# Products inside a chunk, as 64-token halves and in one run per group: a change to the SSD scan of a hybrid decoder trunk

## The chip, the cores and the metric

The kernel runs on one core of one Trainium2 chip. The metric is device time in microseconds (us) of one execution, the median of several runs. A profile of one execution comes with it: records of PE (TensorE's matmuls), PEld (its weight loads), DVE (VectorE), ACT (ScalarE), POOL (GpSimd) and of the DMA queues.

## The reference

One layer of a decoder trunk with two parallel branches, for 16 meta tokens and 2048 real ones at width 1024, all in float32: `u = RMSNorm(h)`, one projection of `u` to all branch inputs and gates, an SSD branch (Mamba-2), a gated linear attention branch (GLA), a gated merge, an output projection, and a last RMSNorm. The change is in the SSD branch. It has 16 heads of 64 channels in 4 groups; the four heads of a group share `bm` and `cm`, of 128 state features each. In chunks of 128 tokens the reference computes

```
da_cum = jnp.cumsum(da, axis=-1)
decay = jnp.exp(jnp.where(causal, seg, -jnp.inf))     # seg[t,s] = da_cum[t] - da_cum[s]
scores = jnp.einsum('bzthn,bzshn->bhzts', cc, bc)
y_diag = jnp.einsum('bhzts,bzsh,bzshp->bzthp', scores * decay, dtc, xc)
states = jnp.einsum('bzshn,bhzs,bzsh,bzshp->bzhpn', bc, decay_to_end, dtc, xc)
# the state is handed on from chunk to chunk: s = chunk_decay * s + states
y_off = jnp.einsum('bzthn,bzhpn,bhzt->bzthp', cc, prev, jnp.exp(da_cum))
y = y_diag + y_off
```

Then `d_skip * xs` is added, the sum is multiplied by `silu(z)`, and each group of 256 channels is normalised by its root mean square over the group. `y_diag`, the product inside a chunk, needs no state; `y_off` and the state do, chunk by chunk.

## The kernel before, in words

There are two stages. The first goes through the 2048 tokens in 4 blocks of 512 (4 chunks each; block 0 has the meta tokens as well, `m0` is then 16) and does projections, the convolution and both scans; it lasts to about 1310 us in the profile. The second does the gates, the branch products and the output product; the change doesn't touch it.

A block's projections are cut into 48 pieces (one more in the last block). After each piece, `step()` (line 1005) calls every running generator once, the oldest first: scans, gates, sums, loads. With the pieces counted from 0, the scan `ssd_scan(o, g)` of group g begins after piece 6(g+1), and the next one six pieces later. So the work of a scan comes in steps, one behind each piece, and the order of PE and SP is the order in which the program writes them (`manual_schedule`, line 1059); that of DVE, ACT and POOL is laid out by a planner from a model of the times.

The steps of one scan (line 630), before the change:

1. The DMA that brings the first chunk's cumulative sums, spread over all partitions (`cb`, line 628).
2. The scores of all four chunks in one bank (line 660), masked by DVE into `scm` (line 662); then `before(0)`.
3. `before(1)`, then `after(0)`. In block 0 the meta tokens' state (line 653, a product on 16 rows) comes as a step ahead of this one.
4. `before(2)`, `after(1)`.
5. `before(3)`, `after(2)`.
6. `after(3)`.
7. The root mean square of each token's group (`rstd_of`), and the scaling of the four chunks on ACT (line 742).
8. (A step later in group 0 of blocks 1 to 3.) Eight transposes (line 749), an eviction with a weight (line 751), and the store of y.

`before(c)` (line 668) transposes the two feature tiles of x and the one of bm (line 676), and makes out of them: `xdt`, x times dt (line 679); `xw`, x times the decay to the chunk's end (line 681); the start of `yt`, x times d_skip (line 682); `bt` (line 685). ACT makes the four decays `dm` of 128 x 128, and DVE multiplies them by the scores (line 692).

`after(c)` (line 695) has on PE, all in fp32: four products of 128 x 128 by 128 x 64, one a head (line 701, `dm[:, h]` is the stationary side and `xdt[:, h]` the moving one); `cf` by the state (line 702); `bt` by `xw` (line 704). Then POOL multiplies the state by the chunk's decay (line 706), DVE adds the new part (line 707), and DVE makes y in four operations (lines 709 to 714): state part times its decay, plus the inside part, plus `yt`, times the gate `zs`. ACT squares and sums (line 721).

Each scan runs beside the projections, `accum` (lines 221 to 225), whose operands are split into two fp32r parts, three matmuls a product. The buffers that matter: PSUM pools `pj` (3 banks), `pt` (3, transposes) and `pc` (2, the scan's products; GLA uses it too). In SBUF, tag `tok4` (5 buffers) holds the z gates, `yt`, v and the gates' `gmt`; `sq` (5) holds `scm` and `dm`, and the GLA scan's tiles; `c1` (8) holds `xdt`, `xw` and `yo`.

Of the kernel before, what the change touches and what calls it, by code (L numbers as in the profile page):

```python
# [8 lines left out]
F32 = mybir.dt.float32  # L9
# [4 lines left out]
ALU = mybir.AluOpType  # L14

P = 128
# [4 lines left out]
NCH = BLK // P  # L21
# [2 lines left out]
NH = 16  # L24
EPS = 1e-6
NWR = 3
NSQ = 5
NT4 = 5
NACT = 8
NC1 = 8  # L30
# [13 lines left out]
def trunk_kernel(ctx: ExitStack, tc: tile.TileContext, xm, xmt, w_feat, w_tok, w_v3, w_zm, w_br, w_o,  # L44
                 cf32, cmsk, pvec, fnw, hvec, gw2, out):
    nc = tc.nc
# [5 lines left out]
    def mk(pool, shape, dt, tag, **kw):  # L52
        cnt[0] += 1
        return pool.tile(shape, dt, tag=tag, name=f"{tag}_{cnt[0]}", **kw)
# [72 lines left out]
    bpool, wk, sm, const = pool1("bpool", 1), pool1("wk", 2), pool1("sm", 4), pool1("const", 1)  # L127
# [4 lines left out]
    pc = ctx.enter_context(tc.tile_pool(name="pc", bufs=2, space=bass.MemoryType.PSUM))  # L132

    def act_tile(dt=F32):
        return mk(wk, [P, 64 + BLK], dt, "act", bufs=NACT)

    def bank(pool, tag):
        return mk(pool, [P, 512], F32, tag)
# [19 lines left out]
    s_ssd = const.tile([P, SG, 256], F32, name="s_ssd")  # L158
# [319 lines left out]
    def gates(o):  # L478
        m0, tt, chunks, g_all = o.m0, o.tt, o.chunks, o.g_all
        ast = (act_tile(F32R) if m0 else mk(wk, [P, BLK], F32R, "sq", bufs=NSQ))[:48, :tt]  # L480
        for a, n in ([(0, META), (m0, BLK)] if m0 else [(0, BLK)]):
# [148 lines left out]
    def ssd_scan(o, g):  # L630
        m0, ci0 = o.m0, o.ci0
        tkd, tkc, wde, ecu, dec = o.tkd, o.tkc, o.wde, o.ecu, o.dec
        x0, x1, bf, cf = o.feats[g]
        fetch_cb(o, g, 0)
        yield
        hs = slice(4 * g, 4 * g + 4)

        def hb(t, n):
            return t.unsqueeze(2).to_broadcast([n, 4, 64])

        if m0:
            ps = bank(pt, "pt")
            for j, f in enumerate((x0, x1, bf)):
                nc.tensor.transpose(ps[:META, j * P:(j + 1) * P], f[:, :META], ident)
            xw = mk(wk, [P, 4, 64], F32, "c1", bufs=NC1)
            nc.vector.tensor_tensor(xw[:META], ps[:META, :256].rearrange("p (a c) -> p a c", c=64),
                                    hb(wde[:META, 0, hs], META), op=ALU.mult)
            btm = mk(wk, [P, P], F32, "bt")
            nc.scalar.activation(btm[:META], ps[:META, 256:384], AF.Copy)

        def meta_state():
            ps = bank(pc, "pc")
            nc.tensor.matmul(ps[:, :256], btm[:META], xw[:META].rearrange("p a c -> p (a c)"),
                             start=True, stop=True)
            nc.vector.tensor_copy(s_ssd[:, g], ps[:, :256])

        sc = bank(pc, "pc")
        for c in range(NCH):
            a = m0 + c * P
            nc.tensor.matmul(sc[:, c * P:(c + 1) * P], bf[:, a:a + P], cf[:, a:a + P], start=True, stop=True)  # L660
        scm = mk(wk, [P, NCH, P], F32, "sq", bufs=NSQ)
        nc.vector.tensor_tensor(scm, sc.rearrange("p (c t) -> p c t", t=P),
                                tri.unsqueeze(1).to_broadcast([P, NCH, P]), op=ALU.mult)
        yt = mk(wk, [P, NCH, 256], F32, "tok4", bufs=NT4)
        ssq = mk(sm, [P, 4], F32, "ssq")
        held = {}

        def before(c):
            a = m0 + c * P
            ci = ci0 + c  # L670
            if c + 1 < NCH:
                fetch_cb(o, g, c + 1)
            cb = cbs.pop((g, c))
            ps = bank(pt, "pt")
            for j, f in enumerate((x0, x1, bf)):
                nc.tensor.transpose(ps[:, j * P:(j + 1) * P], f[:, a:a + P], ident)  # L676
            px = ps[:, :256].rearrange("p (h c) -> p h c", c=64)
            xdt = mk(wk, [P, 4, 64], F32, "c1", bufs=NC1)
            nc.vector.tensor_tensor(xdt, px, hb(tkd[:, ci, hs], P), op=ALU.mult)
            xw = mk(wk, [P, 4, 64], F32, "c1", bufs=NC1)  # L680
            nc.vector.tensor_tensor(xw, px, hb(wde[:, ci, hs], P), op=ALU.mult)
            nc.vector.tensor_tensor(yt[:, c].rearrange("p (h c) -> p h c", c=64), px,
                                    hb(d_skip[:, hs], P), op=ALU.mult)
            bt = mk(wk, [P, P], F32, "bt")
            nc.scalar.activation(bt, ps[:, 256:384], AF.Copy)
            dm = mk(wk, [P, 4, P], F32, "sq", bufs=NSQ)
            with behind() if o.b == 0 else nullcontext():
                for h in range(4):
                    nc.scalar.activation(dm[:, h], cb[:, h], AF.Relu, scale=-1.0,
                                         bias=tkc[:, ci, 4 * g + h:4 * g + h + 1])  # L690
                nc.scalar.activation(dm, dm, AF.Exp, scale=-1.0)
            convd[:] = [nc.vector.tensor_tensor(dm, dm, scm[:, c].unsqueeze(1).to_broadcast([P, 4, P]), op=ALU.mult)]
            held[c] = xdt, xw, bt, dm

        def after(c):
            a = m0 + c * P
            ci = ci0 + c
            xdt, xw, bt, dm = held.pop(c)
            py = bank(pc, "pc")
            for h in range(4):  # L700
                nc.tensor.matmul(py[:, h * 64:(h + 1) * 64], dm[:, h], xdt[:, h], start=True, stop=True)  # L701
            nc.tensor.matmul(py[:, 256:512], cf[:, a:a + P], s_ssd[:, g], start=True, stop=True)  # L702
            pst = bank(pc, "pc")
            nc.tensor.matmul(pst[:, :256], bt, xw.rearrange("p a c -> p (a c)"), start=True, stop=True)  # L704
            sv = s_ssd[:, g].rearrange("p (h c) -> p h c", c=64)
            nc.gpsimd.tensor_tensor(sv, sv, hb(dec[:, ci, hs], P), op=ALU.mult)
            nc.vector.tensor_tensor(s_ssd[:, g], s_ssd[:, g], pst[:, :256], op=ALU.add)
            yo = mk(wk, [P, 4, 64], F32, "c1", bufs=NC1)
            nc.vector.tensor_tensor(yo, py[:, 256:512].rearrange("p (h c) -> p h c", c=64),
                                    hb(ecu[:, ci, hs], P), op=ALU.mult)  # L710
            yof = yo.rearrange("p a c -> p (a c)")
            nc.vector.tensor_tensor(yof, yof, py[:, 0:256], op=ALU.add)
            nc.vector.tensor_tensor(yof, yof, yt[:, c], op=ALU.add)
            nc.vector.tensor_tensor(yt[:, c], yof, o.zs[g][:, c], op=ALU.mult)
            if not m0:
                square(c)

        def square(c):
            with behind() if m0 else nullcontext():
                jk = mk(wk, [P, 256], BF16, "junk", bufs=1)  # L720
                nc.scalar.activation(jk, yt[:, c], AF.Square, accum_out=ssq[:, c:c + 1])

        before(0)
        yield
        if m0:
            meta_state()
            yield
        for c in range(1, NCH):
            before(c)
            if m0 and c > 1:  # L730
                square(c - 2)
            after(c - 1)
            yield
        if m0:
            square(NCH - 2)
        after(NCH - 1)
        yield
        if m0:
            square(NCH - 1)
        r = rstd_of(ssq, 4, 1.0 / 1024)  # L740
        for c in range(NCH):
            nc.scalar.activation(yt[:, c], yt[:, c], AF.Identity, scale=r[:, c:c + 1])
        yield
        if not m0 and not g:
            yield
        for j in range(2):
            ps = bank(pt, "pt")
            for c in range(NCH):
                nc.tensor.transpose(ps[:, c * P:(c + 1) * P], yt[:, c, j * P:(j + 1) * P], ident)
            yo = mk(wk, [P, BLK], F32, "gg", bufs=4)  # L750
            nc.scalar.activation(yo, ps, AF.Identity, scale=hsw[:, 2 * g + j:2 * g + j + 1])
            nc.scalar.dma_start(y_left[0][o.b][2 * g + j], yo)
# [51 lines left out]
    def gla_scan(o, h, last=False):  # L804
# [33 lines left out]
        def level_in(half):  # L838
# [8 lines left out]

            ex = mk(wk, [P, BLK], F32, "sq", bufs=NSQ)
            kq = mk(wk, [P, BLK], F32, "sq", bufs=NSQ)
            ev = view(ex)  # L850
# [68 lines left out]
        for i in range(2):  # L919
            eo = pn[:, :, :, 1 - i]  # L920
            nc.vector.tensor_tensor(eo, eo, halves(q)[:, :, i, :, 1], op=ALU.mult)
            nc.vector.tensor_tensor(eo, eo, halves(k)[:, :, i, :, 0], op=ALU.mult)
        pd = mk(wk, [P, BLK], F32, "sq", bufs=NSQ)
        nc.vector.tensor_tensor(pd, q, k, op=ALU.mult)
# [135 lines left out]
    for b in range(nblk):  # L1060
        o = new_block(b, next_u[b])
# [332 lines left out]
    for si, st in enumerate(stages):  # L1394
        for q in range(0 if si else 12, 28):
            p, j = PS[q // 4], q % 4
# [12 lines left out]
    for key, st in zip(late, (stages[0], stages[-4])):  # L1409
        i, end = begins[stages.index(st)] + 9, begins[stages.index(st) + 1] - 16  # L1410
# [173 lines left out]
```

## Time and profile before

| | us |
|---|---|
| median of 3 runs | 2220.95 |
| lowest and highest | 2220.61, 2226.78 |
| profiled execution, its own time | 2218.94 |
| its span, first to last instruction | 2217.2 |
| matmuls at line 701, busy in all | 64.8 |
| matmuls at line 702 | 42.2 |
| matmuls at line 704 | 38.5 |

The mean granted TensorE clock is 0.999 of full speed. A group's row in the list of groups gives line, engine, operation, tiles out<-in, shape, count, then busy us, mean ns of one, and the idle time ahead of it with what ended it. "128*128 128x64" is a stationary side of 128 rows and 128 columns, and a moving one of 128 rows and 64 columns. Rows of the timeline merge neighbours of one kind: start, length from the first start to the last end, and count. The end of a matmul's record is modelled, and its start may be the moment at which it begins to wait for its weights, so distances between starts say more than durations.

### The profile page before, as it was taken

To read this page: it belongs to the slowest core of one execution; us is meant where nothing else is said; L and a number is where in the kernel's file an instruction comes from. 1 tells how busy PE (TensorE), PEld (TensorE's weight loads), DVE (VectorE), ACT (ScalarE), POOL (GpSimd) and SP (SyncE) were. 2 spreads that over 40 slices of the span, in tenths; PEclk is the share of its full clock that TensorE was granted. 3 is DMA by queue.
4 is the path that set the end of the run, shared out by engine and by line. 5 is a ranking of instruction groups with operands and counts; after the bars stand their busy time and mean duration, and the time that the engine had idled before them with its cause. 6 is when DMAs were issued, how large, how long until landed. Compare 5 with 4: busy or idle time off the path is not lost.

```text
span 2217.2 us, 34962 instructions
## 1 busy us (share of the span) xinstructions
PE 2191.5 (99%) x11789; PEld 1892.3 (85%) x11789; DVE 1570.7 (71%) x2935; ACT 1185.7 (53%) x2767; POOL 689.2 (31%) x689
## 2 busy tenths in 40 slices
PE   7999999999999999999999999999999999999998
PEld 7999999888888888888988888878888888888887
DVE  5775776677667676568677666674789855789876
ACT  5666655475445456545465454464644545554544
POOL 5444432223212122221212100066233274324241
PEclk9999999999999999999999999999999999999999
DMA  9777875767778667778677665376768866687753
GB/s 322 246 230 237 275 264 200 241 209 238 238 251 266 213 213 240 243 251 273 209 222 226 208 219 158 123 262 214 244 228 290 304 225 224 226 299 258 249 183 125
DMA packets 313699, 517.95 MB, mean 234 GB/s; under 512 B 28080, under 2 KB 162480, under 8 KB 313520
## 3 DMA queue, kind: packets, MB, share of 16 engines
q1 hardware_dynamic: 247008, 419.89, 59.0%
q10 hardware_dynamic: 65872, 93.74, 11.5%
q8 instruction: 92, 1.51, 0.3%
q0 software_dynamic: 640, 2.10, 0.2%
q14 instruction: 87, 0.71, 0.1%
HBM read 368.42 MB, written 147.19 MB: 233 GB/s over the span
## 4 chain that ended last, share of the span: by engine, by line
PE 93%; DVE 2%; DMA 2%; ACT 1%; issue 1%; POOL 0%; SPq 0%; POOLq 0%; ACTq 0%; DVEq 0%
PE pj L223 20%; PE pj L225 20%; PE pj L224 20%; PE pt L225 4%; PE pt L224 4%; PE pt L223 4%; PE pc L701 2%; PE pc L223 2%; PE pc L224 2%; PE pc L225 2%; PE pc L866 2%; PE pc L702 1%; PE pc L704 1%; PE pc L974 1%; PE pt L676 1%
## 5 line engine op out<-in xcount | busy, mean ns | idle before, releaser
L223 PE MATMUL pj<-ue,whl 128*128 128x512 f32 (+2 forms) x672 | 235.3, 350 | 1.3 <-ACT acc L608 1.0
L224 PE MATMUL pj<-ue,whl 128*128 128x512 f32 (+2 forms) x672 | 228.0, 339 | 0.0
L225 PE MATMUL pj<-ue,whl 128*128 128x512 f32 (+2 forms) x672 | 227.9, 339 | 0.0
L223 PE MATMUL pj<-uo,whl 128*128 128x512 f32 x512 | 205.6, 402 | 0.0
L225 PE MATMUL pj<-uo,whl 128*128 128x512 f32 x512 | 200.0, 391 | 0.0
L224 PE MATMUL pj<-uo,whl 128*128 128x512 f32 x512 | 199.6, 390 | 0.0
L223 PE MATMUL pj<-b,a 128*128 128x512 f32 (+1 forms) x484 | 187.6, 388 | 0.5 <-DVE io L1297 0.5
L225 PE MATMUL pj<-b,a 128*128 128x512 f32 (+1 forms) x484 | 187.5, 387 | 0.0
L224 PE MATMUL pj<-b,a 128*128 128x512 f32 (+1 forms) x484 | 187.5, 387 | 0.0
L612 DVE SCALAR_TENSOR_TENSOR acc<-cin,hcw,acc 128x512 f32<-128x512 f32 (+1 forms) x192 | 157.1, 818 | 40.6 <-ACT acc L608 39.5
L83 POOL TENSOR_TENSOR wr<-wr 128x256 f32<-128x256 f32 x80 | 65.0, 813 | 370.8 <-DMA wr<-y 155.8
L1179 DVE TENSOR_TENSOR a<-ar,a 128x512 fp32r<-128x512 f32 x160 | 133.3, 842 | 59.0 <-ACT a L1178 58.0
L1150 POOL TENSOR_TENSOR as<-ar,ar 128x512 f32<-128x512 f32 x38 | 59.7, 1572 | 368.4 <-DMA ar<-in_w_br 170.7
L223 PEld LDWEIGHTS pj<-ue,whl 128*128 128x128 f32 x672 | 126.3, 188 | 16.4 <-ACT acc L608 1.6
L225 PEld LDWEIGHTS pj<-ue,whl 128*128 128x128 f32 x672 | 126.4, 188 | 14.1
L224 PEld LDWEIGHTS pj<-ue,whl 128*128 128x128 f32 x672 | 126.9, 189 | 13.3
L186 POOL TENSOR_TENSOR whl<-wr,whl 128x512 fp32r<-128x512 f32 (+1 forms) x76 | 96.6, 1278 | 122.9 <-ACT whl L184 79.6
L1179 DVE TENSOR_TENSOR a<-as,a 128x512 fp32r<-128x512 f32 x120 | 103.5, 863 | 43.9 <-ACT a L1178 40.6
L1178 ACT ACTIVATE a<-ar 128x512 fp32r<-128x512 f32 x160 | 98.9, 624 | 56.0 <-PE pt L225 33.9
L1213 ACT ACTIVATE sn<-pj 128x512 f32<-128x512 f32 x118 | 69.9, 593 | 107.4 <-PE pj L225 68.4
L224 PE MATMUL pt<-b,a 128*128 128x512 f32 x320 | 124.5, 389 | 0.0
L225 PE MATMUL pt<-b,a 128*128 128x512 f32 x320 | 124.5, 389 | 0.0
(335 smaller groups left out, 6447.5 us busy)
## 6 DMA issues: line engine op xcount, KB each, us to landing
whl<-k_s SPq DMA_DIRECT2D x96, 512.0 KB, 3.7
whl<-k_g SPq DMA_DIRECT2D x96, 512.0 KB, 4.2
whl<-k_v SPq DMA_DIRECT2D x36, 512.0 KB, 4.1
wr<-in_w_feat SPq DMA_DIRECT2D x64, 256.0 KB, 4.5
k_s<-whl SPq DMA_DIRECT2D x32, 512.0 KB, 3.8
cb<-cumd SPq DMA_DIRECT2D x64, 256.0 KB, 4.9
y<-gg ACTq DMA_DIRECT2D x64, 256.0 KB, 4.0
k_g<-whl SPq DMA_DIRECT2D x32, 512.0 KB, 3.9
```

Of the source, the lines that this page charges most:

```text
L83: nc.gpsimd.tensor_tensor(o, x, y, op=ALU.subtract)
L186: nc.gpsimd.tensor_tensor(hl[:, 1], raw, hl[:, 0].bitcast(F32), op=ALU.subtract)
L223: nc.tensor.matmul(ps, sh, mh, start=first, stop=False, **kw)
L224: nc.tensor.matmul(ps, sh, ml, start=False, stop=False, **kw)
L225: nc.tensor.matmul(ps, sl, mh, start=False, stop=last, **kw)
L612: convd[:] = [nc.vector.scalar_tensor_tensor(acc, cin[:, k:k + tt], hcw[:, ti, k:k + 1], acc, op0=ALU.mult, op1=ALU.add)]
L701: nc.tensor.matmul(py[:, h * 64:(h + 1) * 64], dm[:, h], xdt[:, h], start=True, stop=True)
L866: nc.tensor.matmul(ps[:, r * P:(r + 1) * P], kq[:, 2 * r * P:(2 * r + 1) * P], kq[:, (2 * r + 1) * P:(2 * r + 2) * P], start=True, stop=True)
L1150: nc.gpsimd.tensor_tensor(s1, a21, a22, op=ALU.add)
L1178: nc.scalar.activation(t[:, 0], src, AF.Copy)
L1179: latest[:] = [nc.vector.tensor_tensor(t[:, 1], src, t[:, 0].bitcast(F32), op=ALU.subtract)]
L1213: nc.scalar.activation(sn, self.ps[n, "a"], AF.Copy)
```

## The change

`after` is taken apart. `off(c)` keeps the two products with the state, now as the two halves of one bank, the update of the state, and `yt[c] +=` state part times decay. `inside()` does the products inside the chunks for all four chunks of the group in one run, two chunks to a bank. Each head's `dm` is cut into two halves of 64 tokens: each is the stationary side of a product of its own (128 rows, 64 columns), and the two write to PSUM partitions 0 to 63 and 64 to 127. DVE adds each bank to two chunks of `yt` at once. The gate is multiplied in for three chunks together and for the last one alone. Steps 3 to 5 have `before(c)` and `off(c - 1)`; step 6 has `inside()`, the gate of three chunks and their squares; step 7 `off(3)` and the last gate; step 8 the last square, the root mean square and the scaling; the transposes are in step 9. `xdt` gets a tag of its own with four buffers, and `sq` has six.

```
-NSQ = 5
+NSQ = 6
...
-            xdt = mk(wk, [P, 4, 64], F32, "c1", bufs=NC1)
+            xdt = mk(wk, [P, 4, 64], F32, "xd", bufs=NCH)
...
-            held[c] = xdt, xw, bt, dm
-
-        def after(c):
+            held[c], intra[c] = (xw, bt), (xdt, dm)
+
+        def off(c):
             a = m0 + c * P
             ci = ci0 + c
-            xdt, xw, bt, dm = held.pop(c)
-            py = bank(pc, "pc")
-            for h in range(4):
-                nc.tensor.matmul(py[:, h * 64:(h + 1) * 64], dm[:, h], xdt[:, h], start=True, stop=True)
-            nc.tensor.matmul(py[:, 256:512], cf[:, a:a + P], s_ssd[:, g], start=True, stop=True)
-            pst = bank(pc, "pc")
-            nc.tensor.matmul(pst[:, :256], bt, xw.rearrange("p a c -> p (a c)"), start=True, stop=True)
+            xw, bt = held.pop(c)
+            ps = bank(pc, "pc")
+            nc.tensor.matmul(ps[:, :256], cf[:, a:a + P], s_ssd[:, g], start=True, stop=True)
+            nc.tensor.matmul(ps[:, 256:], bt, xw.rearrange("p a c -> p (a c)"), start=True, stop=True)
             sv = s_ssd[:, g].rearrange("p (h c) -> p h c", c=64)
             nc.gpsimd.tensor_tensor(sv, sv, hb(dec[:, ci, hs], P), op=ALU.mult)
-            nc.vector.tensor_tensor(s_ssd[:, g], s_ssd[:, g], pst[:, :256], op=ALU.add)
+            nc.vector.tensor_tensor(s_ssd[:, g], s_ssd[:, g], ps[:, 256:], op=ALU.add)
             yo = mk(wk, [P, 4, 64], F32, "c1", bufs=NC1)
-            nc.vector.tensor_tensor(yo, py[:, 256:512].rearrange("p (h c) -> p h c", c=64),
+            nc.vector.tensor_tensor(yo, ps[:, :256].rearrange("p (h c) -> p h c", c=64),
                                     hb(ecu[:, ci, hs], P), op=ALU.mult)
-            yof = yo.rearrange("p a c -> p (a c)")
-            nc.vector.tensor_tensor(yof, yof, py[:, 0:256], op=ALU.add)
-            nc.vector.tensor_tensor(yof, yof, yt[:, c], op=ALU.add)
-            nc.vector.tensor_tensor(yt[:, c], yof, o.zs[g][:, c], op=ALU.mult)
-            if not m0:
-                square(c)
+            nc.vector.tensor_tensor(yt[:, c], yo.rearrange("p a c -> p (a c)"), yt[:, c], op=ALU.add)
+
+        def inside():
+            for c0 in range(0, NCH, 2):
+                py = bank(pc, "pc").rearrange("p (c f) -> p c f", c=2)
+                for i in range(2):
+                    xdt, dm = intra[c0 + i]
+                    for h in range(4):
+                        for ts in (slice(0, 64), slice(64, P)):
+                            nc.tensor.matmul(py[ts, i, h * 64:(h + 1) * 64], dm[:, h, ts], xdt[:, h],
+                                             start=True, stop=True)
+                nc.vector.tensor_tensor(yt[:, c0:c0 + 2], yt[:, c0:c0 + 2], py, op=ALU.add)
+
+        def gate(cs):
+            nc.vector.tensor_tensor(yt[:, cs], yt[:, cs], o.zs[g][:, cs], op=ALU.mult)
...
         for c in range(1, NCH):
             before(c)
-            if m0 and c > 1:
-                square(c - 2)
-            after(c - 1)
+            off(c - 1)
             yield
-        if m0:
-            square(NCH - 2)
-        after(NCH - 1)
-        yield
-        if m0:
-            square(NCH - 1)
+        inside()
+        gate(slice(0, NCH - 1))
+        for c in range(NCH - 1):
+            square(c)
+        yield
+        off(NCH - 1)
+        gate(slice(NCH - 1, NCH))
+        yield
+        square(NCH - 1)
```

More of the change, by code (lines that the diff above doesn't have):

```diff
@@ L665, in ssd_scan @@
         ssq = mk(sm, [P, 4], F32, "ssq")
-        held = {}
+        held, intra = {}, {}
         def before(c):
```

## The prediction

> **What bounds the kernel now.** I read the share of busy time first, then the stretches of the first stage, then PE's own waits, then the chain that ended last.
>
> ```profile
> PE 2191.5 (99%) x11789; PEld 1892.3 (85%) x11789; DVE 1570.7 (71%) x2935; ACT 1185.7 (53%) x2767; POOL 689.2 (31%) x689
> ```
> ```profile
> 80.00:420.00 340.00, 337.27 (x2407) 315.42 (x2407) 246.45 (x495) 208.95 (x544) 135.76 (x125) 0.99 0.71 237
> 420.00:767.00 347.00, 346.97 (x1874) 299.07 (x1873) 239.69 (x529) 182.60 (x474) 79.51 (x108) 1.00 0.75 237
> 767.00:1114.00 347.00, 346.89 (x1873) 298.95 (x1872) 237.37 (x528) 182.37 (x475) 76.36 (x108) 1.00 0.75 238
> 1114.00:1310.00 196.00, 196.00 (x1007) 166.08 (x1006) 139.95 (x295) 108.35 (x276) 37.64 (x59) 1.00 0.69 217
> ```
> ```profile
> PE pt L333 <- DMA cst<-in_cf: 10.0, 1, 10.0
> PE pc L701 <- DVE sq L692: 1.6, 1, 1.6
> ```
> ```profile
> PE 93%; DVE 2%; DMA 2%; ACT 1%; issue 1%; POOL 0%; SPq 0%; POOLq 0%; ACTq 0%; DVEq 0%
> ```
>
> The columns of the stretches are length, then PE, PEld, DVE, ACT and POOL busy, granted clock, DMA share, GB/s. The four stretches are the four blocks of 512 tokens while the scans run. In the second, PE is busy for 346.97 of 347.00 us, DVE for 239.69, and the DMA engines for 0.75 of their time. PE waits for one scan product once, for 1.6 us. So the first stage is as long as PE's own work, in the order written out for it, and a microsecond taken out of that work leaves the total until DVE or a transfer becomes late. DVE has 347.00 − 239.69 = 107 us to spare in a block, far more than is at stake here.
>
> "Busy" hides something, though: a matmul that waits in PE for its weights counts as busy. So I read the price of a step from distances between starts, of loads (PEld) and of matmuls (PE), around one chunk of the scan.
>
> ```profile
> 86.45 0.37 PEld L676 LDWEIGHTS pt<-cst,act 128*128 128x128 f32 x3
> 86.79 0.97 PEld L701 LDWEIGHTS pc<-c,sq 128*128 128x128 f32 x8
> 87.68 0.30 PEld L702 LDWEIGHTS pc<-s_ssd,act 128*128 128x128 f32 x2
> 88.01 0.41 PEld L704 LDWEIGHTS pc<-c,bt 128*128 128x128 f32 x2
> 88.44 0.19 PEld L223 LDWEIGHTS pj<-ue,whl 128*128 128x128 f32 x1
> ```
> ```profile
> 86.57 0.49 PE L676 MATMUL pt<-cst,act 128*128 128x128 f32 x3
> 86.89 1.00 PE L701 MATMUL pc<-c,sq 128*128 128x64 f32 x8
> 87.73 0.65 PE L702 MATMUL pc<-s_ssd,act 128*128 128x256 f32 x2
> 88.22 0.60 PE L704 MATMUL pc<-c,bt 128*128 128x256 f32 x2
> 88.77 0.28 PE L224 MATMUL pj<-ue,whl 128*128 128x256 f32 x1
> 88.89 0.28 PE L225 MATMUL pj<-ue,whl 128*128 128x256 f32 x1
> ```
> ```profile
> L701 PE MATMUL pc<-c,sq 128*128 128x64 f32 x512 | 64.8, 270 | 1.6 <-DVE sq L692 1.6
> ```
>
> The code calls L701 256 times (16 groups, 4 chunks, 4 heads) and the group has 512 records: one fp32 call is two pairs of load and matmul. In a chunk, 8 loads of L701 take from 86.79 to 87.68, 0.89 us, 0.111 each. Three matmuls of 128 columns at L676 take from 86.57 to 86.89, 0.107 each, so one of 64 columns should stream for about half, 0.054 (estimate). Load and matmul overlap, the load is twice as long, and the array idles half the time: L701 is bound by loading 128 weight columns for 64 moving ones. At L704 it is the reverse: its second matmul starts with the load of L223, at 88.44, 0.22 after the first, so 256 columns hide their loads.
>
> **What leaves.** L701 goes from every chunk. L702 then follows the transposes of L676, and its first load can lie beside the last of them, as L701's did (86.79, against L676's last matmul at about 86.78). That takes out 0.89 us per chunk, 64 × 0.89 = 57.0 us.
>
> **What comes in.** For each group one run of 32 calls, 64 pairs of a load of 64 columns and a matmul of 64. Nothing in this trace shows two matmuls on different halves of the array, so I bound it. First, does a narrow load cost less?
>
> ```profile
> L473 PEld LDWEIGHTS pt<-cst,tkc x16: 88/90/93, 45.8 to 1114.7; 128*16 128x16 f32 x16
> ```
> ```profile
> L676 PEld LDWEIGHTS pt<-cst,act x192: 137/140/144, 73.7 to 1296.4; 128*128 128x128 f32 x192
> ```
>
> These are loads for transposes, of 16 and of 128 columns: 90 and 140 ns at the median. The duration has a fixed part and one that goes with the columns; I take half of 0.111, 0.056 us, for 64 columns (estimate). The lower bound is that the halves run side by side throughout: 32 × 0.056 = 1.78 us a group, 28.5 in all. The middle bound is one half after the other, each load still beside a matmul: 64 × 0.056 = 3.56 us, 57.0 in all, exactly what was removed. The upper bound is that no load lies beside any matmul: 64 × (0.056 + 0.054) = 7.0 us, 112.6 in all. I take the lower bound: the rows show PE overlapping two pieces of work wherever they use different parts of it (L704's loads beside L702's matmuls), and the halves have neither columns of the array nor PSUM partitions in common.
>
> The Trainium skill, in "TensorE: Matmul & The Clock Gate", section "The mechanism" of Part 3, states that a weight load overlaps matmuls in flight only where the row groups differ. Both halves here use all 128 rows, so by that rule the upper bound would hold. On the undivided array the rows above disagree: the loads of L704 start at 88.01, during L702's matmuls (87.73 to 88.38), all on 128 rows. No row shows it on halves.
>
> **The switch.** The one other use of a part of the array in this kernel is the meta tokens' product on 16 rows.
>
> ```profile
> 79.76 0.28 PE L225 MATMUL pj<-ue,whl 128*128 128x272 f32 x1
> 79.97 0.69 PE L653 MATMUL pc<-c,bt 16*128 16x256 f32 x2
> 80.60 0.38 PE L223 MATMUL pj<-ue,whl 128*128 128x256 f32 x1
> 80.82 0.29 PE L224 MATMUL pj<-ue,whl 128*128 128x256 f32 x1
> 80.94 0.28 PE L225 MATMUL pj<-ue,whl 128*128 128x256 f32 x1
> ```
>
> From 79.76 to 80.94 are 1.18 us. The work in it is one matmul of 272 columns (0.125, scaled up from the next), two fp32 ones of 256 columns at 0.22, and two of 256 at 0.12 (88.77 to 88.89): 0.81 us. So going in and out costs 0.37 to 0.38 us: PE runs empty, and the next load has nothing to hide behind. For 16 groups: 6.1 us if halves of the columns behave like parts of the rows, 0 if they don't. I take 6.1, the only row there is.
>
> **The rest.** Vector work gets shorter.
>
> ```profile
> L709 DVE TENSOR_TENSOR c<-pc,ecu 128x256 f32<-128x256 f32 x64 | 26.5, 415 | 34.1 <-PE pc L702 34.1
> L712 DVE TENSOR_TENSOR c<-c,pc 128x256 f32<-128x256 f32 x64 | 26.2, 410 | 0.4
> L713 DVE TENSOR_TENSOR c<-c,tok 128x256 f32<-128x256 f32 x64 | 28.1, 440 | 0.4
> L714 DVE TENSOR_TENSOR tok<-c,tok 128x256 f32<-128x256 f32 x64 | 32.6, 509 | 1.1
> L662 DVE TENSOR_TENSOR sq<-pc,cst 128x512 f32<-128x512 f32 x16 | 10.9, 683 | 2.0 <-PE pc L660 2.0
> ```
>
> Per group 16 operations of 256 elements (L709 to L714, about 0.44 us at the mean, 7.1 us) become 9 of 256 (3.7), 2 of 512 at 0.68 and one of 768 at about 0.95 (estimate, by 0.27 for each further 256): 6.0 us. That is 18 us less of DVE work in all, worth nothing while DVE has a quarter of each block free; if that cover were gone, it would help. The squares on ACT are as many as before, three of them together; no transfer is added. Each scan takes one step more: the last chunk's state product moves a step back, and with it the row scale, the transposes and the store of y. A step is 347 / 48 pieces = 7.2 us; the stored y is read in a later block, so that is hidden. What waits is buffers. `inside` needs both banks of pc; the younger was last read one step earlier. It needs all four dm, the last made a step earlier too, as before. If one were late, PE's next projection would queue behind it.
>
> Sum: −57.0 + 28.5 + 6.1 = −22.4 us. The profiled execution took 2218.94 us (span 2217.2 and 1.7 around it), 2.0 below the median of 2220.95; so 2196.5 for such an execution and about 2199 for the median after.
>
> **The rivals.**
>
> *One half after the other* (0.18): the middle bound. For it: no row shows two matmuls at once, and the code gives both pairs of one half before those of the other, so a queue that keeps strictly to the order finds few neighbours on different halves. Then −57.0 + 57.0 + 6.1 = +6.1: 2227. In between lie orders that overlap only where the half changes: at half the gain, about −8, 2213; I count them with the forecast.
>
> *Loads laid bare* (0.10): the upper bound, −57.0 + 112.6 + 6.1 = +62 us: 2283. It decides where the mean distance of the 1024 new pairs exceeds (57.0 − 6.1) / 1024 = 0.050 us; the forecast has 0.028. Against it stand L702 to L704, where loads are hidden.
>
> *One step longer, and buffers run out* (0.08): with the added step, yt of one group is alive until the second chunk of the next has begun. At the 13th step of a block that makes five tok4 tiles at once (two yt, two z tiles, a gate tile) of five. If DVE has to wait to write the new yt, the transposes' bank stays taken and PE waits. Nothing now shows such a wait; the nearest price is the 1.6 us at L701. At 12 places between groups that is 19 us: −3, 2218.
>
> **How the numbers follow.** The forecast has 0.64: −22.4, from −28.5 (no cost of switching) to −8. About 0.3%, 6.7 us, is what a measurement of this kernel can tell from no change. Faster: 0.64, and 0.02 of the buffers. Within: 0.15 of the serial halves (+6.1 lies close to the border) and 0.05 of the buffers. Slower: 0.10, 0.03 and 0.01. The range goes from 2190 (−28.5 and a little of DVE's relief) to 2229, the serial halves; the bare loads are left out. The likeliest case alone has 2192 to 2213.
>
> **What would show it.** In the changed trace the new matmuls should start 0.028 us apart in the mean, a group's run taking 1.8 us plus an entry and an exit of some 0.2; at 0.056 (3.6 us) the halves are serial, at 0.11 the loads are bare. Loads should last about 0.14 instead of 0.19. L702 should start within 0.11 of the last transpose. PE's waits should show no new line at the scan's matmuls or transposes, and a block should be some 5.6 us shorter. I am wrong if PE's distances come out as here and the blocks don't shrink; then a wait has taken the place.

## The result and the profile after

The changed kernel takes 2209.86 us (median of 6 runs, 2207.38 to 2213.43) against 2220.78 before on the same chip (6 runs); the ratio is 0.995, with a 95% interval of 0.9935 to 0.9965. That is 10.9 us less, about half of what the sum had forecast. The profiled execution took 2209.51 us, its span is 2207.7.

On PE the change does what was meant. The first fence below is from the list of groups after the change, the second is PE's timeline around one run of products in block 1.

```profile
L700 PE MATMUL pc<-s_ssd,act 128*128 128x256 f32 x128 | 38.4, 381 | 0.0
L717 PE MATMUL pc<-xd,sq 128*64 128x64 f32 x1024 | 33.4, 224 | 0.0
L717 PEld LDWEIGHTS pc<-xd,sq 128*64 128x64 f32 x1024 | 31.2, 138 | 5.2 <-issue 4.9
```

```profile
524.56 0.39 PE L224 MATMUL pj<-uo,whl 128*128 128x512 f32 x1
524.78 0.39 PE L225 MATMUL pj<-uo,whl 128*128 128x512 f32 x1
525.10 2.09 PE L717 MATMUL pc<-xd,sq 128*64 128x64 f32 x64
527.12 0.50 PE L223 MATMUL pj<-uo,whl 128*128 128x512 f32 x1
527.45 0.39 PE L224 MATMUL pj<-uo,whl 128*128 128x512 f32 x1
527.68 0.39 PE L225 MATMUL pj<-uo,whl 128*128 128x512 f32 x1
```

There are twice as many records as L701 had, and they are busy for half as long: 33.4 us for 64.8. In the timeline 64 pairs last 2.09 us, of which the last matmul's record is 0.22, so 63 distances take 1.87, 0.030 each. In the single records the starts lie about 7 and 52 ns apart in turn: two matmuls at a time. The record of a load of 64 columns lasts 138 ns, that of a load of 128 columns at L701 before 192 (median). The whole insertion is read from the neighbours: L224 starts at 527.45, so L223 ahead of it streamed from about 527.22 (0.23 for 512 columns, as from 527.45 to 527.68); L225 ahead of the run streamed until 525.01 (524.78 + 0.23). So the run costs 2.21 to 2.22 us: 64 × 0.030 = 1.89 for its pairs, and some 0.33 for the ways in and out.

Now the blocks. These are the score products (L660) of group 0, at the beginning of blocks 1, 2 and 3, and those of the last group; first before, then after.

```profile
448.48 1.05 PE L660 MATMUL pc<-act,act 128*128 128x128 f32 x8
795.54 1.05 PE L660 MATMUL pc<-act,act 128*128 128x128 f32 x8
1142.68 1.05 PE L660 MATMUL pc<-act,act 128*128 128x128 f32 x8
1274.52 1.06 PE L660 MATMUL pc<-act,act 128*128 128x128 f32 x8
```
```profile
452.98 1.05 PE L660 MATMUL pc<-act,act 128*128 128x128 f32 x8
795.30 1.05 PE L660 MATMUL pc<-act,act 128*128 128x128 f32 x8
1138.11 1.05 PE L660 MATMUL pc<-act,act 128*128 128x128 f32 x8
1265.81 1.05 PE L660 MATMUL pc<-act,act 128*128 128x128 f32 x8
```

From block 1 to block 2 the changed kernel needs 342.32 us for 347.06, from 2 to 3 342.81 for 347.14: a block is 4.3 to 4.7 us shorter. But block 1 begins 4.5 us later than before. Block 0, which was to gain 5.6 us as the others, lost 4.5. (1.0 of it is there before any scan has begun: the first L660 starts at 72.4 before and at 73.4 after.) PE's waits after the change (who waited for whom, total, times, longest) say where to look:

```profile
PE pj L223 <- ACT acc L608: 4.3, 4, 2.1
PE pc L223 <- DVE c L969: 2.8, 3, 2.1
PE pt L676 <- ACT s_gla L785: 2.4, 1, 2.4
PE pc L701 <- ACT bt L685: 1.9, 3, 0.7
```

Before, the longest wait of a scan's or a projection's matmul in this part was 1.6 us. The longest new one, and what follows it, in the timeline:

```profile
232.94 0.55 PE L676 MATMUL pt<-cst,act 128*128 128x128 f32 x3 [2.44 <-ACT s_gla L785]
...
235.20 0.63 PE L224 MATMUL pj<-ue,whl 128*128 128x512 f32 x1
235.63 0.63 PE L225 MATMUL pj<-ue,whl 128*128 128x512 f32 x1
236.06 0.63 PE L223 MATMUL pj<-ue,whl 128*128 128x512 f32 x1
...
237.42 0.39 PE L224 MATMUL pj<-ue,whl 128*128 128x512 f32 x1
```

The matmuls behind the wait stand 0.43 us apart where others of 512 columns stand 0.23 apart: PE's clock is down to about half for some 3.4 us (a stretch laid inside it, 233.6 to 236.9, has a granted clock of 0.50). The stretches of 20 us, before and then after, show it as the granted clock (the number behind POOL's busy time):

```profile
220.00:240.00 20.00, 20.00 (x143) 18.34 (x142) 13.49 (x27) 15.05 (x39) 9.91 (x9) 1.00 0.98 345
300.00:320.00 20.00, 19.31 (x154) 18.45 (x153) 15.43 (x34) 15.39 (x46) 6.04 (x5) 1.00 0.74 240
```
```profile
220.00:240.00 20.00, 17.56 (x113) 15.56 (x112) 10.06 (x23) 15.05 (x40) 9.28 (x10) 0.91 0.90 316
300.00:320.00 20.00, 17.93 (x127) 17.26 (x126) 18.37 (x39) 13.60 (x42) 6.55 (x5) 0.91 0.81 274
```

At 0.91 a stretch of 20 us loses 1.8 us more. So two waits of 2.4 and 2.1 us cost about 4 us each. The waits for L608 at 97 and 107 us (1.05 and 2.06 us) are new too. They stand in place of one of 1.62 us for the decays (L692), and the granted clock from 100 to 120 us is 0.91 in both kernels.

What the 2.4 us wait for is the eviction of v (L785, ACT), which frees a bank of pt. These are the transposes of the scan's tail and what follows them, first before, then after:

```profile
222.15 1.03 PE L749 MATMUL pt<-cst,tok 128*128 128x128 f32 x8
225.61 1.25 ACT L751 ACTIVATE gg<-pt,hsw 128x512 f32<-128x512 f32 x2
```
```profile
229.46 1.04 PE L756 MATMUL pt<-cst,tok 128*128 128x128 f32 x8
232.53 0.36 ACT L785 ACTIVATE s_gla<-pt 16x256 f32<-16x256 f32 x1
233.32 1.23 ACT L758 ACTIVATE gg<-pt,hsw 128x512 f32<-128x512 f32 x2
```

Before, the tail's two banks were written a step ahead of v's and empty again at 226.9; the next chunk's transposes (L676) found a free bank at 230.75 and did not wait. After, the tail's transposes come between the end of v's product and L676. So all three banks of pt are taken, and L676 starts when the oldest, v's, is empty.

### The profile page after: what moved, and what is told of

Same layout as the page of the kernel before. It is cut to its first block, busy times and chain, and to the rows that moved or that the text cites. A ratio compares the mean times of both kernels' runs of the same rounds, so it can differ in the third digit from the quotient of the medians.

```text
span 2207.7 us, 35845 instructions
## 1 busy us (share of the span) xinstructions
PE 2174.5 (98%) x12301; PEld 1867.9 (85%) x12301; DVE 1553.8 (70%) x2871; ACT 1188.5 (54%) x2767; POOL 693.8 (31%) x689
## 3 DMA queue, kind: packets, MB, share of 16 engines
q10 hardware_dynamic: 65872, 93.74, 11.6%
## 4 chain that ended last, share of the span: by engine, by line
PE 86%; DVE 4%; ACT 3%; DMA 3%; POOL 1%; issue 1%; SPq 1%; POOLq 0%; ACTq 0%; DVEq 0%
PE pj L223 19%; PE pj L225 19%; PE pj L224 19%; PE pt L225 4%; PE pt L224 4%; PE pt L223 4%; PE pc L223 2%; PE pc L224 2%; PE pc L225 2%; PE pc L873 2%; PE pc L717 1%; PE pc L701 1%; PE pc L981 1%; PE pc L700 1%; DVE acc L612 1%
## 5 line engine op out<-in xcount | busy, mean ns | idle before, releaser
L223 PE MATMUL pj<-ue,whl 128*128 128x512 f32 (+2 forms) x672 | 236.7, 352 | 2.3 <-ACT acc L608 2.2
L224 PE MATMUL pj<-ue,whl 128*128 128x512 f32 (+2 forms) x672 | 228.9, 341 | 0.0
L225 PE MATMUL pj<-ue,whl 128*128 128x512 f32 (+2 forms) x672 | 228.5, 340 | 0.0
L223 PE MATMUL pj<-uo,whl 128*128 128x512 f32 x512 | 206.0, 402 | 0.0
L225 PE MATMUL pj<-uo,whl 128*128 128x512 f32 x512 | 199.9, 390 | 0.0
L224 PE MATMUL pj<-uo,whl 128*128 128x512 f32 x512 | 199.5, 390 | 0.0
L223 PE MATMUL pj<-b,a 128*128 128x512 f32 (+1 forms) x484 | 187.4, 387 | 0.5 <-DVE io L1304 0.5
L224 PE MATMUL pj<-b,a 128*128 128x512 f32 (+1 forms) x484 | 187.4, 387 | 0.0
L225 PE MATMUL pj<-b,a 128*128 128x512 f32 (+1 forms) x484 | 187.4, 387 | 0.0
L83 POOL TENSOR_TENSOR wr<-wr 128x256 f32<-128x256 f32 x80 | 69.7, 871 | 332.2 <-DMA wr<-y 142.0
L223 PEld LDWEIGHTS pj<-ue,whl 128*128 128x128 f32 x672 | 127.2, 189 | 18.3 <-ACT acc L608 3.1
L186 POOL TENSOR_TENSOR whl<-wr,whl 128x512 fp32r<-128x512 f32 (+1 forms) x76 | 102.6, 1357 | 122.0 <-ACT whl L184 93.4
L225 PEld LDWEIGHTS pj<-ue,whl 128*128 128x128 f32 x672 | 127.1, 189 | 14.4
L224 PEld LDWEIGHTS pj<-ue,whl 128*128 128x128 f32 x672 | 127.7, 190 | 13.3
L224 PE MATMUL pt<-b,a 128*128 128x512 f32 x320 | 124.5, 389 | 0.0
L225 PE MATMUL pt<-b,a 128*128 128x512 f32 x320 | 124.5, 389 | 0.0
```

What stands on the lines that cost most here:

```text
L83: nc.gpsimd.tensor_tensor(o, x, y, op=ALU.subtract)
L186: nc.gpsimd.tensor_tensor(hl[:, 1], raw, hl[:, 0].bitcast(F32), op=ALU.subtract)
L223: nc.tensor.matmul(ps, sh, mh, start=first, stop=False, **kw)
L224: nc.tensor.matmul(ps, sh, ml, start=False, stop=False, **kw)
L225: nc.tensor.matmul(ps, sl, mh, start=False, stop=last, **kw)
```

## The experiments

Theory A: the halves work as forecast, 1.34 us less a group (3.56 − 2.22), 21.4 us in all, and the other half of the gain is lost in block 0, to waits that come with the scan's new order. Theory B: the halves bring little, and the gain is from the grouping.

**Whole columns in the same run.**

```
-                        for ts in (slice(0, 64), slice(64, P)):
+                        for ts in (slice(0, P),):
```

> The run of all four chunks stays, but each head's product is one of 128 columns again, as at L701 before. Theory A (the gain comes from two halves working at once): a group's run has 32 pairs at 0.111 us, 3.56 us, without a switch, where the halves took 2.22 us from the end of the matmul ahead to the start of the one behind. That is 1.34 us more a group, 21 us in all: about 2231. Theory B (the gain comes from the grouping, from fewer and larger DVE operations and products out of the chain of the state): about 2210, as with the halves.

2230.84 us (2230.39 to 2235.51), ratio 1.0055 (1.0041 to 1.0068). The run:

```profile
529.69 3.68 PE L717 MATMUL pc<-xd,sq 128*128 128x64 f32 x32
533.17 0.48 PE L223 MATMUL pj<-uo,whl 128*128 128x512 f32 x1
```

B falls. The run alone, with the same order of all else, is 10 us slower than the kernel before. PE has the same products to do as before, so the delay is the price of the new order by itself, and most of it is there when block 1 begins:

```profile
456.22 1.05 PE L660 MATMUL pc<-act,act 128*128 128x128 f32 x8
1286.09 1.05 PE L660 MATMUL pc<-act,act 128*128 128x128 f32 x8
```

456.22 against 448.48: 7.7 us later; at the last group 11.6 later (1286.09 against 1274.52). The wait for L785 is there with whole columns too (3.0 us), and so are those for L608 (3.1 in all): neither is made by the halves.

**The halves not alternating.**

```
-                    for h in range(4):
-                        for ts in (slice(0, 64), slice(64, P)):
+                    for ts in (slice(0, 64), slice(64, P)):
+                        for h in range(4):
```

> The same products in another order: in each chunk the four heads' first halves, then the four second halves, so that neighbours in the queue are mostly on the same half. If PE takes loads and matmuls in the order of the queue and overlaps only neighbours on different halves: about 0.056 us a pair instead of 0.030, 3.6 us a run, some 26 us more in all, 2236. If each half works off its own queue that reaches far ahead (8 pairs here): 0.030 a pair, 2210 as it is.

2220.77 us (2214.37 to 2224.23), ratio 0.9994 (0.9982 to 1.0006): the gain is gone. Neither number came out:

```profile
528.70 2.69 PE L717 MATMUL pc<-xd,sq 128*64 128x64 f32 x64
```

2.69 less 0.22 is 2.47 us for 63 distances, 0.039 each. Single starts follow as 54, 4, 54, 58, 6, 53, 54, 4 ns. In strict order only every eighth distance, where the half changes, could be a short one; here 6 of 16 are. So PE seems to run ahead of the order to the other half, but not far enough to keep both halves busy through eight pairs of one. That is argued, as the records don't name the half; how far it reaches, and by which rule, stays open. That the order of the calls decides is shown: 2.47 − 1.87 = 0.6 us a run, 9.6 us over 16 runs, and the medians differ by 10.9 (2220.77 and 2209.86). (Part of that difference is block 0's: the wait for L785 is 4.3 us in this profile, for 2.4.)

**Quarters.**

```
-                        for ts in (slice(0, 64), slice(64, P)):
+                        for ts in [slice(k, k + 32) for k in range(0, P, 32)]:
```

> Four quarters of 32 tokens instead of two halves: 128 pairs a group. If the pairs of the halves are bound by streaming 64 moving columns (0.054 us on each part, parts side by side), four parts give 0.015 us a pair, 1.9 us a run, and the time stays at about 2210. If 0.030 us a pair is what PE needs to start one, the run takes 128 x 0.030 = 3.8 us, 1.9 more a group, 31 us in all: 2240.

2212.76 us (2207.65 to 2214.61), ratio 0.9963 (0.995 to 0.9975).

```profile
529.15 1.99 PE L717 MATMUL pc<-xd,sq 128*32 128x64 f32 x128
```

128 pairs in 1.99 − 0.22 = 1.77 us, 0.014 each; starts lie 7, 7, 6 and 36 ns apart. Not the start of an instruction bounds the halves but the streaming of 64 moving columns, some 0.055 us on each part, parts side by side. A finer cut gives 0.09 us a run, not half. The median is 2.9 above the changed kernel's, within the spread of the two; the wait for L785 is 4.3 us in this profile.

**Block 0 in its old order.** Its four scans are done by `after(c)`, put back as it was; blocks 1 to 3 are as changed.

```
-            off(c - 1)
+            (after if m0 else off)(c - 1)
...
-        inside()
...
+        if m0:
+            square(NCH - 2)
+            after(NCH - 1)
+        else:
+            inside()
```

> Block 0 has its four scans as before the change (whole columns, chunk by chunk, no step more); blocks 1 to 3 have the halves. Theory A: the changed kernel lost its gain of 4 groups in block 0, and more, to waits that the moved tail of the scan brought there (block 1 begins 4.5 us later than before, not 5 us earlier); with the old order block 0 is as long as before, blocks 1 to 3 keep their 13.7 us, and the total is about 2207, 3 below the changed kernel. Rival (block 0's loss is from the switch of the array, or has nothing to do with the scan's order): either it comes back in another block, or block 0 only loses its 4 x 1.3 us of gain, and the total is 2213 to 2215.

2204.17 us (2203.95 to 2206.04), ratio 0.9932 (0.9919 to 0.9946): 5.7 us faster than the changed kernel, more than forecast. Block 1 begins at

```profile
446.36 1.05 PE L660 MATMUL pc<-act,act 128*128 128x128 f32 x8
```

6.6 us earlier than with the change, though block 0 gave up its halves. It is also 2.1 earlier than in the kernel before, whose order it has there. The wait of 1.62 us for the decays at 105 us is in both profiles, but before the change the granted clock behind it was 0.91 (100 to 120 us), and here 1.00. So some 1.8 us of the difference between these two profiles is not the change's.

**The halves at their old place.** The kernel before, with only this edit:

```
-                nc.tensor.matmul(py[:, h * 64:(h + 1) * 64], dm[:, h], xdt[:, h], start=True, stop=True)
+                for ts in (slice(0, 64), slice(64, P)):
+                    nc.tensor.matmul(py[ts, h * 64:(h + 1) * 64], dm[:, h, ts], xdt[:, h], start=True, stop=True)
```

> The kernel before the change with one edit: each product inside a chunk is cut into two halves, chunk by chunk, at its old place. No step, no buffer and no DVE operation changes, so the waits of block 0 should be those of before. With a switch to halves and back at 0.33 us (what a run of 64 pairs took beyond its pairs, 2.22 - 1.89), a chunk's 16 pairs take 16 x 0.030 + 0.33 = 0.80 instead of 0.89: 64 x 0.09 = 6 us less, 2215. If the switch costs nothing here (the cost of a run being something else), 0.48 a chunk: 26 us less, 2194.

2215.68 us (2213.76 to 2221.03), ratio 0.9982 (0.9973 to 0.9991), 4.2 less than the kernel before.

```profile
565.95 0.39 PE L225 MATMUL pt<-whl,uo 128*128 128x512 f32 x1
566.26 0.69 PE L702 MATMUL pc<-c,sq 128*64 128x64 f32 x16
566.88 0.70 PE L703 MATMUL pc<-s_ssd,act 128*128 128x256 f32 x2
567.41 0.59 PE L705 MATMUL pc<-c,bt 128*128 128x256 f32 x2
```

16 pairs last 0.69 − 0.22 = 0.47 us, as in the run, but the way in and out is paid in each chunk: 0.80 us from the end of L225 (566.18) to the streaming of L703 (566.98, two of 0.216 ahead of L705). That is the use of the run: 16 switches in place of 64, at 0.33 us 16 us of difference. 64 × 0.09 = 5.8 us were expected; the interval, 2.0 to 6.0, still has them, and this profile waits 0.5 us longer for the decays and 0.4 for L963.

**The last state product in block 0 without a step of its own.** It comes ahead of the run:

```
+        if m0:
+            off(NCH - 1)
         inside()
...
-        yield
-        off(NCH - 1)
+        if not m0:
+            yield
+            off(NCH - 1)
```

> The changed kernel, but in block 0 the last chunk's product with the state comes in the step of the run, ahead of it, so that the tail of each scan stays in its old step; blocks 1 to 3 as changed. If it is the moved tail that meets the eviction of v in block 0 (PE waited 2.4 us for L785 there and ran about 3.4 us at half clock behind it, some 1.7 us more): 4 us less, 2205 to 2206. If block 0 loses through the altered work in the earlier steps (the waits for L608 at 97 and 107 us): 2209 to 2211, unchanged.

2218.48 us (2216.26 to 2222.38), ratio 0.9992 (0.9983 to 1.0001): a miss. The wait for L785 is gone, and the two banks of pc have taken its place:

```profile
PE pc L717 <- DVE tok L719: 3.6, 1, 3.6
PE pc L717 <- DVE c L706: 3.0, 2, 2.7
```

Three tiles of pc in one step, and two banks: the second half of the run waits until DVE has emptied `off`'s bank. So the added step has a use, and this run doesn't tell what it costs.

**Only the added step.** The kernel of old_block0, with the scan's tail in block 0 one step later:

```
+        if m0:
+            yield
         square(NCH - 1)
```

> The kernel of old_block0 (2204.2) with one thing more: in block 0 the row scale and the transposes of each scan come one step later, as in the changed kernel, all else in block 0 as before the change. If the later tail is what costs: the wait for the eviction at L785's place comes back, 4 us or more, 2208 to 2211. If not: 2204 to 2205.

2210.57 us (2207.49 to 2213.96), ratio 0.9951 (0.9936 to 0.9966), 6.4 more than old_block0. The profile has the very wait of the changed kernel, and the half clock behind it. The third fence shows what ACT did ahead of that eviction:

```profile
PE pt L676 <- ACT s_gla L814: 2.5, 1, 2.5
```
```profile
220.00:240.00 20.00, 17.52 (x118) 15.71 (x118) 13.85 (x28) 14.14 (x37) 8.78 (x8) 0.91 0.99 342
```
```profile
232.37 0.63 ACT L316 ACTIVATE acc<-acc 128x512 f32<-128x512 f32 x1 [2.31 <-DMA acc<-in_xm]
233.00 0.36 ACT L814 ACTIVATE s_gla<-pt 16x256 f32<-16x256 f32 x1
```
```profile
452.23 1.05 PE L660 MATMUL pc<-act,act 128*128 128x128 f32 x8
```

Block 1 begins 5.9 us later than in old_block0 (452.23 against 446.36). The old products with the later tail make the wait; the new products have no part in it. How long it lasts depends on when ACT comes to v: here ACT stood for 2.31 us until the DMA of the next block's input had landed, with v's eviction behind it; in the changed kernel it stood 0.43 there and had other work. The waits for L608 are gone in this run as in old_block0, so the later tail does not make those; the new order of the steps ahead of it does.

**Versions that might beat both.** Quarters in blocks 1 to 3 on top of old_block0:

```
-                        for ts in (slice(0, 64), slice(64, P)):
+                        for ts in [slice(k, k + 32) for k in range(0, P, 32)]:
```

> The best candidate: block 0 in its old order as in old_block0, quarters of 32 tokens in blocks 1 to 3. The quarters' run was 1.775 us against 1.863 for the halves: 12 x 0.09 = 1 us less than old_block0 at best, 2203. If the 256 instructions more a group cost something elsewhere, it is 2204 or slower.

2207.72 us (2204.82 to 2208.9), ratio 0.9939 (0.9927 to 0.9952): no gain that can be measured; the median is 3.6 above old_block0's and the intervals overlap. (In this profile the granted clock is 0.83 from 100 to 120 us, behind the same wait of 1.62 us.) The halves in block 0, chunk by chunk, on top of old_block0, in `after(c)`:

```
-                nc.tensor.matmul(py[:, h * 64:(h + 1) * 64], dm[:, h], xdt[:, h], start=True, stop=True)
+                for ts in (slice(0, 64), slice(64, P)):
+                    nc.tensor.matmul(py[ts, h * 64:(h + 1) * 64], dm[:, h, ts], xdt[:, h], start=True, stop=True)
```

> old_block0 (2204.2) with one edit: block 0's products, chunk by chunk at their old place, are cut into halves as in per_chunk. 16 chunks at 0.09 us less: 1.4 us, 2202.8, if the waits of block 0 stay as they are. The saving lies within the noise, so the profile decides: 16 pairs of a chunk in about 0.8 us with the switch.

2204.97 us (2204.48 to 2207.62), ratio 0.9939 (0.9927 to 0.9952): no difference that can be measured; the wait for the decays in group 0 (1.6 us in old_block0) is 2.2 us here, and the granted clock behind it 0.91.

For the last version, old_block0 with one more edit, look at the first chunk of group 1 in the changed kernel, where L701 waits for its own stationary side:

```profile
503.60 0.60 PE L700 MATMUL pc<-s_ssd,act 128*128 128x256 f32 x2
504.81 0.70 PE L701 MATMUL pc<-c,bt 128*128 128x256 f32 x2 [0.62 <-ACT bt L685]
```

```
-            nc.scalar.activation(bt, ps[:, 256:384], AF.Copy)
+            if o.b and g == 1 and c == 0:
+                nc.vector.tensor_copy(bt, ps[:, 256:384])
+            else:
+                nc.scalar.activation(bt, ps[:, 256:384], AF.Copy)
```

> old_block0 with one edit: in group 1 of blocks 1 to 3 the first chunk's bt (L685) is brought out of PSUM by DVE and not by ACT, where ten relus of the decays stand ahead of it. If that order on ACT is what the first state product waits for (three waits of 0.6 us, 1.8 in all): they go, 2202.4. If DVE is as late, or the planner lays the rest out otherwise: 2204 or slower.

2201.59 us (2201.07 to 2203.52), ratio 0.9924 (0.991 to 0.9937), the kernel before at 2218.49 on that chip. The three waits are gone; the longest wait of a scan product left is the old one in block 0 (its line is L704 in this kernel):

```profile
PE pc L704 <- DVE sq L695: 1.6, 1, 1.6
```

It is the fastest kernel of this study, some 17 us below the kernel before. That it is faster than old_block0 rests on the waits; the intervals overlap. Two more waits of old_block0's profile are not there, 1.1 us at L456 and 1.0 at L223 for L996, and the edit isn't shown to be the cause of that.

## Why the prediction was right, and where its sum was wrong

**What leaves, 57.0 us: right.** With whole columns in the run, block 1 takes 348.83 us (456.22 to 805.05) for 347.06 before. Of the 1.8 more, 1.3 are waits (0.6 for `bt`, 0.7 for L969), so the products cost in the run about what they cost in the chunks. But L701 before had hidden something: the eviction of `bt`. In the first chunk of group 1 of blocks 1 to 3 it is late, because ACT has ten relus ahead of it, and with the 0.89 us of products gone PE waits 0.62 to 0.70 us: 1.9 us in three places, shown by `bt_dve`. The prediction named no wait that the removed work covered.

**What comes in, 28.5 us: right in kind and nearly in size.** The halves do run side by side, 0.030 us a pair for 0.028, and the narrow load takes less. The serial halves and the bare loads are out: a run of 64 pairs on halves that share all 128 rows streams for 1.9 us, where the serial halves would have taken 3.56 and the bare loads 7.0. So the rule from "TensorE: Matmul & The Clock Gate" in the Trainium skill that was weighed against the change (Part 3, "The mechanism") does not hold in this trace, on halves either.

**The switch, 6.1 us: right.** It is 0.33 us a run, 5.3 in all, where 0.38 was taken from the meta tokens' product; `per_chunk` pays it four times as often and gains 4.2 us, where 5.8 follows from it.

**The rest: here the sum failed.** Of 21.4 us (16 × 1.34) about 10.9 came out. The step that failed is "Each scan takes one step more … so that is hidden." The prediction looked at who reads y, at the banks of pc and at the buffers, but not at the banks of pt that the moved transposes would hold, nor at when ACT would empty the bank they wait behind. In block 0 they now come right behind v's product. With two banks for them and one for v, the next chunk's transposes wait for the eviction of v (L785). `step0` shows with the old products that the later tail makes this wait: 2.5 us, then the half clock, 6 us in all. That the order of the banks is the reason is read from the traces; no run has another number of banks. The row scaling, which moved as well, is not the reason: in `step0` it is done at 220.4 us, ten microseconds ahead of the wait. Block 0 came out 9.9 us off the sum (5.4 to gain, 4.5 lost), and the traces have a place for them: 4.2 for this wait with its half clock; 3.2 for the wait for L969 with its own (2.1 where it was 0.7, and 1.8); 1.5 for the waits for L608, which the new order of the earlier steps makes (3.1 in place of 1.6 for the decays, the half clock behind them being there before too); and the 1.0 by which the first scan began later.

The rival of the added step had the mechanism (PE waits for a bank of pt) but the wrong owner (a tok4 buffer, which no trace shows as a wait) and the wrong price (1.6 us at 12 places, for one place in block 0 at about 4). The forecast's range for its likeliest case, 2192 to 2213, reached as far as 2209.86 only because it allowed for halves that overlap in part. They overlap fully, so that the time lies in the range is luck: the halves gave what was summed up, and waits that nobody had put into the sum took half of it.

With the old order in block 0 the sum comes out nearly for the rest: 12 × 1.34 = 16.1 us was to be had, less 1.8 of the waits for `bt`, 14.3; old_block0 took 16.6 less than the kernel before beside it, whose runs spread from 2217.87 to 2222.7. The profiles put some 1.8 of the 2.3 between these down to the half clock at 105 us that one has and the other has not. What is not settled: the wait in block 0 at 305 us, for DVE's L969, 2.1 us where it was 0.7. It is 0.9 in `step0`, so the later tail alone doesn't make it, and its longest is 0.8 in `whole` and in `quarters`, whose steps come in the same order as the changed kernel's. No run here isolates its cause.

## What to carry to other kernels

A product of 64 moving columns was bound here by loading its 128 weight columns (0.111 us a pair). Cutting it by output partitions let PE work on the two parts side by side (0.030 us a pair of half the size), as long as neighbours in the order lay on different parts and one run was long enough to carry the switch of 0.33 us. On an engine that is always busy, take the price from distances between starts, and check for each removed or moved step what it covered and what it meets at its new place: which buffers and banks it holds there, and every engine that has to empty them. A stall of 2.1 to 2.4 us on PE cost nearly twice its length here where the half clock followed.

## What the runs showed of the hardware that had not been expected

After each of its waits of 2.1 to 2.4 us in block 0 the changed kernel ran at about half its clock for some 3.4 us: matmuls of 512 columns 0.43 us apart for 0.23, a granted clock of 0.91 over 20 us. A wait of 1.05 us (97 us in the changed kernel) did not show it in the matmuls behind it. But the length of the wait does not settle it. In `whole` and in `apart` the same wait of 2.07 us for L608 left the clock up:

```profile
100.00:120.00 20.00, 17.93 (x145) 16.92 (x145) 17.08 (x31) 13.84 (x31) 7.14 (x7) 1.00 0.57 177
```

That is `whole`. And behind one and the same wait of 1.62 us for the decays the granted clock over 100 to 120 us was 0.91 before the change, 1.00 in old_block0 and 0.83 in `quarters_old0`. What decides it is not shown; it moves two profiles apart by up to 3.4 us (0.17 of 20 us) with the waits alike.

Four quarters of the columns started within 20 ns of each other and took 0.055 us together. And with eight pairs of one half in a row the distance was 0.039 us a pair, between 0.030 and the 0.056 estimated for strict order.
